# RWKV core: the transposed 32x32 blocks of the join, read off PSUM by VectorE instead of multiplied by TensorE

## The chip, the cores and the metric

The kernel runs on one core of one Trainium2 chip. The metric is the device time of one execution, in microseconds (us): the median of several runs. Five engines work side by side, each through a queue of its own in order: TensorE (PE in the profile, its weight loads are PEld), VectorE (DVE), ScalarE (ACT), GpSimd (POOL) and SyncE (SP, which here issues the transfers).

## The reference

Four layers of token mixers over 256 context and 256 latent tokens of 1024 features: retention, mLSTM, RWKV-7, retention. Only the third is touched. Its scan is, for 16 heads of 64 features and in both directions:

```python
def step(S, inp):
    rt, wt, kt, vt, at, bt = inp
    sa = jnp.einsum('bhij,bhj->bhi', S, at)
    S = S * wt[:, :, None, :] + sa[..., None] * bt[:, :, None, :] + vt[..., None] * kt[:, :, None, :]
    return S, jnp.einsum('bhij,bhj->bhi', S, rt)
```

## The kernel before

All matrices of the other layers are float32, split into two parts and multiplied three times (lines 255 to 257 of the profile). The RWKV core works on chunks of 64 tokens. Within a chunk the term with `sa` couples the tokens, so that a triangular 64x64 system stands for each head and direction; it is solved by inverting unit triangular matrices, first of 16, then of 32, then of 64 rows.

There are eight chunks per direction, so eight stages n = 0 to 7. In a stage the core handles four units (two directions, two halves of the heads), by these functions:

- `prep` (P) loads k, kk and r and makes decays and keys: `L1284` on TensorE, `L1289` to `L1296` and `L1310` on ScalarE, `L1292`, `L1293`, `L1300`, `L1301`, `L1305`, `L1307` on VectorE, the rest on GpSimd.
- `grams1` (G) multiplies keys by each other (`L1327`) and copies the diagonal 32x32 blocks into `AD` and the lower left ones into `off` (ScalarE, in the profile `AD<-g` and `q<-g`); `grams2` (H) does the same for another pair (`L1343`).
- `solve` (I) inverts the 16-row blocks of all heads at once on VectorE (`L1372` to `L1383`), and leaves them turned, as `O1` (the tile `AD`), and not turned, as `O2`.
- `whole` (J), called the join from here on, makes 32-row and then 64-row inverses. It has 16 blocks b for each of four quarters of the partitions, so each of its first steps is 64 small matmuls of 32x32. `L1394` multiplies the off-diagonal 16-row part by `O2`, `L1395` (VectorE) adds the identity and gives `Pm`. `L1399` multiplies `O1` by `Pm`: the 32-row inverse, in PSUM; four ScalarE copies (one helper line, `L1197`) put it into `M` (in the profile the tile `bdB`). `L1405` multiplies the same pair the other way round, `Pm` by `O1`: the same blocks transposed, in another PSUM bank, and a ScalarE copy makes them `MT`. `L1411` multiplies `off` by `M`; two copies, one on ScalarE and one on VectorE, make `Q` (in the profile `Pm<-ps`). `L1417` multiplies `MT` by `Q`, and two more copies complete `M`. `L1423` multiplies by `M` and gives `G`, which the steps need.
- `step` (T) advances the state of one unit: `L1438`, `L1440` and, after a copy, `L1447`, `L1449`, `L1450`.
- `ada` (A) makes the scales of the fourth layer, `L307`, in the last two stages, from weights that stream in as `adaw`.

The program text runs P, G, H, I and J of stage n, then A of stage n and T of stage n-1. The order on each engine is not the text's: a scheduler lays all instructions out on a time line of its own and sorts every engine's queue by that, so that rows of T, P, G and H stand between those of a join. An edit anywhere in the core therefore moves other rows too. The PSUM pool behind `bank("ps")` has two buffers.

The profile's records count two matmuls and two weight loads for each float32 matmul of the program, so that the 64 matmuls of one step of a join are 128 matmul records.

Of the kernel before, what the change touches and what calls it, by code (L numbers as in the profile page):

```python
# [131 lines left out]
class Net:  # L132
# [1051 lines left out]
    def rk_core(self, es, e0, K, B, xd, h, xx, p1, p0):  # L1184
        nc = self.nc
        mm = nc.tensor.matmul
# [10 lines left out]
        copy = lambda o, x: nc.scalar.activation(o, x, ACT.Copy)  # L1197
# [188 lines left out]
        def whole(units, O1, O2, los):  # L1386

            quarters = [(32 * q, slice(32 * q, 32 * q + 32)) for q in range(4)]
            part = lambda name: tl(name, 1, 16, 32)
            wide = lambda: bank("ps").rearrange("p q t -> p (q t)").rearrange("p (b t) -> p b t", t=32)  # L1390
            ps, Pm = wide(), part("Pm")
            for b in range(16):
                for o, r in quarters:
                    mm(ps[r, b], los[b // 8][r, :, b % 8], O2[r, :, b], start=True, stop=True, tile_position=(o, o))  # L1394
            nc.vector.tensor_tensor(out=Pm, in0=ps, in1=K["m16"][:, 2].unsqueeze(1).broadcast_to([128, 16, 32]), op=OP.add)  # L1395
            ps, MT = wide(), part("MT")
            for b in range(16):
                for o, r in quarters:
                    mm(ps[r, b], O1[r, :, b], Pm[r, b], start=True, stop=True, tile_position=(o, o))  # L1399
            for q, (o, r) in enumerate(quarters):  # L1400
                (vcopy if q % 2 else copy)(M[r, :, q // 2, 32 * (q % 2):32 * (q % 2) + 32], ps[r])
            ps = wide()
            for b in range(16):
                for o, r in quarters:
                    mm(ps[r, b], Pm[r, b], O1[r, :, b], start=True, stop=True, tile_position=(o, o))  # L1405
            copy(MT, ps)
            ps, Q = wide(), part("Pm")
            low = [(64 * h, slice(64 * h, 64 * h + 32), 64 * h + 32, slice(64 * h + 32, 64 * h + 64)) for h in range(2)]
            for b in range(16):
                for h, (o, r, o2, r2) in enumerate(low):  # L1410
                    mm(ps[r2, b], units[b // 4]["off"][r, b % 4], M[r, b, h, 0:32], start=True, stop=True, tile_position=(o, o2))  # L1411
            for h, (o, r, o2, r2) in enumerate(low):
                (qcopy if h else copy)(Q[r2], ps[r2])
            ps = wide()
            for b in range(16):
                for o, r, o2, r2 in low:
                    mm(ps[r2, b], MT[r2, b], Q[r2, b], start=True, stop=True, tile_position=(o2, o2))  # L1417
            for h, (o, r, o2, r2) in enumerate(low):
                (qcopy if h else copy)(M[r2, :, h, 0:32], ps[r2])
            for m, u in enumerate(units):  # L1420
                ps = bank("ps")
                for p in range(4):
                    mm(ps[:, p], cat(M[:, 4 * m + p]), u["RB"][:, p], start=True, stop=True)  # L1423
                u["G"] = tl("G", GN, 4, 128)
                (gcopy if m % 2 else copy)(u["G"], ps)
# [124 lines left out]
        def J(n, m):  # L1550
            whole(U[n], *O[n])
# [142 lines left out]
```

## Time and profile before

| | |
|---|---|
| median of 3 runs | 2121.55 us (2121.2 to 2126.33) |
| the profiled execution | 2119.65 us |
| its span, first to last instruction | 2117.9 us |
| busy: TensorE / VectorE / ScalarE / GpSimd | 93% / 60% / 43% / 20% of the span |
| the joins | eight, from 1265 us to about 1665 us of the span |

The profile says of each engine when it was busy and, for idle time, what released the instruction that ended it. "issue" as a releaser means that nothing that the profile shows was waited for. [...]

### The profile page before, as it was taken

How to read it: one execution, taken by the hardware profiler on the slowest of the kernel's cores; microseconds unless marked ns; L12 is line 12 of the kernel's file. 1: busy time of each engine (PE TensorE's matmuls, PEld its weight loads, DVE VectorE, ACT ScalarE, POOL GpSimd, SP SyncE). 2: the span in 40 equal slices, each digit the busy share in tenths (PEclk: the TensorE clock that was granted, in tenths of full speed). 3: DMA queues.
4: the chain of work that ended last, by engine and by line, in shares of the span. 5: the costliest groups of instructions: out<-in, count | busy, mean ns of one | idle time of the engine just before them, and what ended most of it. 6: DMA issues, size and time to landing. Idle time of an engine off the chain costs nothing.

```text
span 2117.9 us, 41647 instructions
## 1 busy us (share of the span) xinstructions
PE 1968.9 (93%) x17146; PEld 1676.3 (79%) x17146; DVE 1260.9 (60%) x2296; ACT 919.6 (43%) x1841; POOL 430.5 (20%) x459
## 2 busy tenths in 40 slices
PE   6999999999999989989699998999999898999996
PEld 5888887887777868777567987888898676999995
DVE  4463544446646266676867536777766466665554
ACT  3241423233434555342435436666665342444433
POOL 1000000004300143340700402332322033311001
PEclk9999999999999989999899998999999999999998
DMA  9332434331554564443135521112234630233331
GB/s 302 107 119 92 138 100 130 105 120 60 189 179 130 171 195 134 149 125 112 61 124 166 168 69 48 40 52 60 70 87 135 202 123 1 90 121 110 120 108 42
DMA packets 241550, 246.40 MB, mean 116 GB/s; under 512 B 30992, under 2 KB 200080, under 8 KB 241360
## 3 DMA queue, kind: packets, MB, share of 16 engines
q1 hardware_dynamic: 241360, 243.73, 36.8%
q8 instruction: 135, 2.21, 0.4%
q14 instruction: 55, 0.45, 0.1%
HBM read 216.29 MB, written 27.39 MB: 115 GB/s over the span
## 4 chain that ended last, share of the span: by engine, by line
PE 73%; DVE 12%; DMA 5%; ACT 5%; issue 3%; POOL 2%; SPq 0%; ACTq 0%; DVEq 0%; POOLq 0%
PE pp L255 15%; PE pp L256 15%; PE pp L257 15%; PE po L256 2%; PE ps L82 2%; PE g L1327 2%; PE po L257 2%; PE po L255 2%; PE ps L307 1%; DMA raw<-ada_w 1%; DVE wl L239 1%; PE g L1343 1%; PE pp L1450 1%; PE ps L255 1%; PE pp L1447 1%
## 5 line engine op out<-in xcount | busy, mean ns | idle before, releaser
L239 DVE TENSOR_TENSOR wl<-wraw,wh 128x1024 fp32r<-128x1024 f32 x216 | 269.3, 1248 | 196.1 <-ACT wh L237 186.7
L237 ACT ACTIVATE wh<-wraw 128x1024 fp32r<-128x1024 f32 x216 | 228.5, 1059 | 271.8 <-PE pp L256 129.0
L255 PE MATMUL pp<-hA,wh 128*128 128x512 f32 (+1 forms) x704 | 255.9, 366 | 8.1 <-DVE rp L526 3.0
L256 PE MATMUL pp<-hB,wh 128*128 128x512 f32 (+1 forms) x704 | 255.4, 364 | 0.0
L257 PE MATMUL pp<-hA,wl 128*128 128x512 f32 (+1 forms) x704 | 255.2, 364 | 0.1
L255 PE MATMUL pp<-zh,wh 128*128 128x512 f32 (+1 forms) x620 | 216.7, 352 | 6.5 <-ACT zh L287 6.0
L257 PE MATMUL pp<-zh,wl 128*128 128x512 f32 (+1 forms) x620 | 212.3, 343 | 0.0
L256 PE MATMUL pp<-zl,wh 128*128 128x256 f32 (+1 forms) x512 | 170.8, 334 | 4.4 <-DVE zl L288 2.9
L366 DVE SCALAR_TENSOR_TENSOR x<-pp,mod,x 128x256 f32<-128x256 f32 x192 | 87.0, 480 | 137.2 <-PE pp L257 136.9
L255 PEld LDWEIGHTS pp<-hA,wh 128*128 128x128 f32 x704 | 132.8, 189 | 33.1 <-PE pp L257 3.6
L257 PEld LDWEIGHTS pp<-hA,wl 128*128 128x128 f32 x704 | 133.5, 190 | 24.3 <-issue 1.6
L256 PEld LDWEIGHTS pp<-hB,wh 128*128 128x128 f32 x704 | 133.6, 190 | 22.5 <-issue 1.7
L255 PE MATMUL pp<-wh,hA 128*128 128x256 f32 x512 | 146.4, 287 | 2.0 <-ACT wh L237 1.9
L255 PEld LDWEIGHTS pp<-zh,wh 128*128 128x128 f32 x620 | 119.0, 192 | 34.1 <-ACT zh L287 6.9
L256 PE MATMUL pp<-wl,hA 128*128 128x256 f32 x512 | 145.1, 284 | 0.5 <-DVE wl L239 0.5
L257 PE MATMUL pp<-wh,hB 128*128 128x256 f32 x512 | 145.0, 284 | 0.0
L257 PEld LDWEIGHTS pp<-zh,wl 128*128 128x128 f32 x620 | 119.4, 193 | 19.3 <-issue 6.7
L256 PEld LDWEIGHTS pp<-zl,wh 128*128 128x128 f32 x512 | 99.2, 194 | 18.6 <-issue 5.4
L255 PEld LDWEIGHTS pp<-wh,hA 128*128 128x128 f32 x512 | 97.5, 191 | 5.9 <-issue 2.6
L256 PEld LDWEIGHTS pp<-wl,hA 128*128 128x128 f32 x512 | 97.4, 190 | 1.4 <-DVE wl L239 0.8
L257 PEld LDWEIGHTS pp<-wh,hB 128*128 128x128 f32 x512 | 97.5, 190 | 0.0
L288 DVE TENSOR_TENSOR vl<-pp,vh 128x256 fp32r<-128x256 f32 x64 | 26.9, 421 | 82.4 <-ACT vh L287 82.4
(520 smaller groups left out, 4687.4 us busy)
## 6 DMA issues: line engine op xcount, KB each, us to landing
wraw<-ret_w_in SPq DMA_DIRECT2D x96, 512.0 KB, 3.8
wraw<-ada_w SPq DMA_DIRECT2D x56, 512.0 KB, 4.0
wraw<-ret_w_out SPq DMA_DIRECT2D x32, 512.0 KB, 3.5
wraw<-ml_w_in SPq DMA_DIRECT2D x32, 512.0 KB, 3.8
wraw<-rk_w_rkvg SPq DMA_DIRECT2D x32, 512.0 KB, 3.7
adaw<-ada_w SPq DMA_DIRECT2D x48, 256.0 KB, 4.4
raw<-ada_w SPq DMA_DIRECT2D x16, 512.0 KB, 7.5
wraw<-ml_w_out SPq DMA_DIRECT2D x16, 512.0 KB, 4.5
```

Of the source, the lines that this page charges most:

```text
L82: nc.tensor.matmul(self.sums[32 * j:32 * j + 32, n * HALF:n * HALF + HALF], net.ones[:, 0:32], src, start=c < 4 and n == 0, stop=c >= 4 an ...
L237: nc.scalar.activation(h, t, ACT.Copy)
L239: (nc.gpsimd if self.nsplit % 4 in self.psplit else nc.vector).tensor_tensor(out=l, in0=t, in1=f(h), op=OP.subtract)
L255: mm(ps, lhs[0], rhs[0], start=start, stop=False)
L256: mm(ps, lhs[0], rhs[1], start=False, stop=False)
L257: mm(ps, lhs[1], rhs[0], start=False, stop=stop)
L288: (eng or self.nc.vector).tensor_tensor(out=l, in0=src, in1=f(h), op=OP.subtract)
L307: nc.tensor.matmul(ps[32 * j:32 * j + 32, 0:m].rearrange("p (b q) -> p b q", b=nb), self.csil[:, k, :], raws[k // n][:, k % n, j], start=k ...
L366: self.nc.vector.scalar_tensor_tensor(out=x, in0=ps, scalar=self.gate(i, c, st), in1=x, op0=OP.mult, op1=OP.add)
L1327: mm(g[:, p, 0:192], cat(u["bb"][:, p]), W[:, p], start=True, stop=True)
L1343: mm(g[:, p, 0:192], cat(u["kb"][:, p]), W[:, p], start=True, stop=True)
L1447: mm(f_[0:m, p], AK[:, p, 64:64 + m], cat(V[:, p]), start=True, stop=False)
```

## The change

The second set of 64 matmuls of each join, its PSUM bank and its ScalarE copy go. In their place one VectorE instruction reads the result of the first set from PSUM, turns each 32x32 block and writes `MT`. What `MT` holds is the same.

```diff
                     mm(ps[r, b], O1[r, :, b], Pm[r, b], start=True, stop=True, tile_position=(o, o))
             for q, (o, r) in enumerate(quarters):
                 (vcopy if q % 2 else copy)(M[r, :, q // 2, 32 * (q % 2):32 * (q % 2) + 32], ps[r])
-            ps = wide()
-            for b in range(16):
-                for o, r in quarters:
-                    mm(ps[r, b], Pm[r, b], O1[r, :, b], start=True, stop=True, tile_position=(o, o))
-            copy(MT, ps)
+            nc.vector.transpose(MT.rearrange("p b t -> p (b t)"), ps.rearrange("p b t -> p (b t)"))
             ps, Q = wide(), part("Pm")
```

Later lines move up by four: `L1411` becomes `L1407`, `L1417` `L1413`, `L1423` `L1419`, and the steps' `L1438`, `L1440`, `L1447`, `L1449`, `L1450` become `L1434`, `L1436`, `L1443`, `L1445`, `L1446`. The transpose is `L1402`. The scheduler's order changes in the whole core, and hardly outside it.

TensorE's queue at join 2, before:

```order
L1438 MATMUL pp<-bdB,AK 64x128
L1399 MATMUL ps<-Pm,AD_10515 32x32 x64
L1405 MATMUL ps<-AD_10515,Pm 32x32 x64
L1327 MATMUL g_13022<-W_11336,bdA 128x192 x4
L1440 MATMUL pp<-S_11351,W_10503 64x128
...
L1411 MATMUL ps<-bdB,q 32x32 x32
```

and now:

```order
L1327 MATMUL g_12827<-W_11336,bdA 128x192 x2
L1399 MATMUL ps<-Pm,AD_10515 32x32 x64
L1327 MATMUL g_12827<-W_11336,bdA 128x192 x2
L1434 MATMUL pp<-bdB,AK 64x128
L1436 MATMUL pp<-S_11351,W_10503 64x128
...
L1443 MATMUL pp<-bdB,AK 128x128
L1407 MATMUL ps<-bdB,q 32x32
```

The gram matmuls and the steps now follow the first block of 64 at once, and stand between it and the block that reads `M`.

TensorE's queue at join 6, before (no other row stood between the blocks there):

```order
L1284 MATMUL g_15787<-ta,ca_9162 128x128
L1399 MATMUL ps<-Pm,AD_10515 32x32 x64
L1405 MATMUL ps<-AD_10515,Pm 32x32 x64
L1411 MATMUL ps<-bdB,q 32x32 x32
L1450 MATMUL pp<-bdB,G 128x128
```

and now:

```order
L1399 MATMUL ps<-Pm,AD_10515 32x32 x64
L1443 MATMUL pp<-bdB,AK_11350 128x128
L1445 MATMUL pp<-S_11357,W_11337 128x128
L1446 MATMUL pp<-bdB,G 128x128
...
L1284 MATMUL g_15332<-ta,ca_9162 128x128
L1407 MATMUL ps<-bdB,q 32x32
L1327 MATMUL g_15371<-W_11336,bdA 128x192 x4
L1407 MATMUL ps<-bdB,q 32x32 x31
```

Twelve matmuls of a step have moved from behind `L1411` to before it; join 1 is alike, with seven.

VectorE's queue at join 2, before:

```order
L1395 TENSOR_TENSOR Pm<-ps,cm_9172 128x512
L1305 TENSOR_TENSOR bdA<-kk,em 64x4x2x64
L1453 TENSOR_TENSOR S_11357<-pp,Dc 64x4x64 x2
L1292 TENSOR_SCALAR em<-em 128x512
L1293 SCALAR_TENSOR_TENSOR em<-creset,em 128x512
L1300 SCALAR_TENSOR_TENSOR W_11337<-kk,eL_10512 128x8x64
```

and now:

```order
L1395 TENSOR_TENSOR Pm<-ps,cm_9172 128x512
L1449 TENSOR_TENSOR S_11357<-pp,Dc 64x4x64 x2
L1292 TENSOR_SCALAR em<-em 128x512
L1293 SCALAR_TENSOR_TENSOR em<-creset,em 128x512
L1402 STREAM_TRANSPOSE MT<-ps 128x512
L1300 SCALAR_TENSOR_TENSOR W_11337<-kk,eL_10512 128x8x64
```

The transpose, which waits for `L1399`, has come in ahead of the row that makes the next `W`, on which a gram waits.

## Rows read from the trace of the kernel before

**Rows 1.** The page: busy time, share of the span and instructions of each engine.

```profile
PE 1968.9 (93%) x17146; PEld 1676.3 (79%) x17146; DVE 1260.9 (60%) x2296; ACT 919.6 (43%) x1841; POOL 430.5 (20%) x459
```

**Rows 2.** Busy time by stage: start:end, length, each engine, PEclk, DMA share, GB/s.

```profile
1418.00:1474.00 56.00, 53.53 (x852) 49.34 (x848) 44.02 (x87) 37.59 (x98) 17.11 (x15) 0.94 0.22 63
sum 405.00, PE 370.16 PEld 333.85 DVE 266.48 ACT 237.41 POOL 111.64; mean PE 46.27 PEld 41.73 DVE 33.31 ACT 29.68 POOL 13.96
```

**Rows 3.** The same view, from the solve of stage 3 to its end.

```profile
1398.60:1417.80 19.20, 18.05 (x164) 16.48 (x163) 18.32 (x49) 6.51 (x19) 0.00 (x0) 1.00 0.21 57
```

**Rows 4.** Groups by line, 1265 to 1670: busy, mean ns, idle before and releasers.

```profile
L1405 PE MATMUL ps<-AD,Pm 32*32 32x32 f32 x1024 | 18.1, 229 | 12.6 <-issue 12.6
L1399 PE MATMUL ps<-Pm,AD 32*32 32x32 f32 x1024 | 16.5, 222 | 1.2 <-issue 0.8 <-DVE Pm L1395 0.3
L1411 PE MATMUL ps<-bdB,q 32*32 32x32 f32 x512 | 11.7, 207 | 7.1 <-ACT bdB L1197 6.5 <-issue 0.6
L1197 ACT ACTIVATE MT<-ps 128x512 f32<-128x512 f32 x8 | 4.8, 597 | 3.0 <-PE ps L1405 2.7
```

**Rows 5.** TensorE's time line at joins 2 and 5: start, length, row, idle before.

```profile
1376.62 2.02 PE L1399 MATMUL ps<-Pm,AD 32*32 32x32 f32 x128
1378.46 1.42 PE L1405 MATMUL ps<-AD,Pm 32*32 32x32 f32 x84
1381.52 0.85 PE L1405 MATMUL ps<-AD,Pm 32*32 32x32 f32 x44 [1.65 <-issue]
1382.30 2.69 PE L1327 MATMUL g<-W,bdA 128*128 128x192 f32 x8
...
1393.27 1.57 PE L1327 MATMUL g<-W,bdA 128*128 128x192 f32 x8 [0.26 <-ACT RB L1197]
...
1537.20 0.76 PE L1405 MATMUL ps<-AD,Pm 32*32 32x32 f32 x38
...
1540.69 0.80 PE L1450 MATMUL pp<-bdB,G 128*128 128x128 f32 x2
```

**Rows 6.** Windows of 1 us after that gap (columns as in Rows 2).

```profile
1382.00:1383.00 1.00, 1.00 (x27) 0.91 (x16) 0.64 (x1) 0.93 (x3) 0.94 (x2) 0.79 0.73 219
1383.00:1384.00 1.00, 1.00 (x5) 1.00 (x4) 1.00 (x3) 0.61 (x2) 0.84 (x2) 0.50 0.00 0
...
1386.00:1387.00 1.00, 1.00 (x16) 0.83 (x16) 0.00 (x0) 0.97 (x4) 0.00 (x0) 1.00 0.00 0
```

**Rows 7.** The page: the instruction queue with the most bytes.

```profile
q8 instruction: 135, 2.21, 0.4%
```

**Rows 8.** TensorE's time line at join 7, and around the lone block of join 4.

```profile
1641.88 1.95 PE L1399 MATMUL ps<-Pm,AD 32*32 32x32 f32 x122 [0.83 <-issue]
...
1647.00 2.02 PE L1405 MATMUL ps<-AD,Pm 32*32 32x32 f32 x123 [3.10 <-issue]
...
1474.33 2.23 PE L1394 MATMUL ps<-O,q 32*32 32x32 f32 x128 [1.00 <-DVE O L1383]
...
1477.68 0.27 PE L1450 MATMUL pp<-bdB,G 128*128 128x128 f32 x1 [0.81 <-issue]
```

**Rows 9.** TensorE and ScalarE at join 0 and join 1.

```profile
1280.59 1.92 PE L1411 MATMUL ps<-bdB,q 32*32 32x32 f32 x64 [4.26 <-ACT bdB L1197]
1334.37 1.66 PE L1411 MATMUL ps<-bdB,q 32*32 32x32 f32 x64 [1.45 <-ACT bdB L1197]
1331.94 2.37 ACT L1197 ACTIVATE bdB<-ps 32x512 f32<-32x512 f32 x4
```

**Rows 10.** Groups by line on VectorE: transposes and a copy out of PSUM.

```profile
L1382 DVE STREAM_TRANSPOSE AD<-LS 128x1024 f32<-128x1024 f32 x7 | 8.7, 1245 | 0.2
L1383 DVE STREAM_TRANSPOSE O<-LS 128x1024 f32<-128x1024 f32 x7 | 13.4, 1914 | 0.0
L310 DVE STREAM_TRANSPOSE lnt<-g 128x128 f32<-128x128 f32 x6 | 1.9, 310 | 5.0 <-PE g L307 5.0
L1198 DVE COPY G<-ps 128x512 f32<-128x512 f32 x15 | 10.2, 680 | 6.5 <-PE ps L1423 6.5
```

## The prediction

> **What bounds the kernel now.** I read the page first: TensorE is busy 93% of the span [rows 1]. The change lies in the eight joins alone, so next comes the view by stage: over the 405 us that hold them TensorE is busy 370 us, VectorE 266 and ScalarE 237 [rows 2]; in stage 3 it is 53.5 of 56 us for TensorE and 44 for VectorE. A microsecond taken from TensorE's queue there should shorten the stage unless VectorE's solve sets the pace. It does for one stretch: between the first instruction of the solve and its end, 19.2 us, VectorE is busy 18.3 us [rows 3], and the block L1394 that follows it can wait for it (1.00 us at join 4) [rows 8]. But the solve starts from grams that stand behind the join before it in TensorE's queue, so a shorter join starts it earlier as well.
>
> Then the groups by line. L1405, which the change removes, is busy 18.1 us in all and has 12.6 us of idle time before or inside it that nothing visible ends, "issue" [rows 4]. Its twin L1399 has only 1.2 us. The time line of join 2 shows what that is: L1399 runs 128 records in 2.02 us, L1405 runs 84, stops for 1.65 us, and runs the other 44 [rows 5]. [...] L1327 x8 takes 2.69 us there and 1.57 us ten microseconds later at full clock [rows 5].
>
> **What the gap is.** The page counts 17146 matmuls and 17146 loads [rows 1], and 135 packets with 2.21 MB on one instruction queue [rows 7]: 254 records and 16.4 KB a packet. Two blocks of 64 in a row are 512 records. At join 7 the engine stops inside L1399 and again inside L1405, with 122 matmuls, one more and five between (and as many loads): one packet apart [rows 8]. The small matmuls eat a packet in some 1.9 us, and the next is not there. The lone block L1394 has such a gap in one join of eight, two matmuls behind its end, 0.81 us [rows 8]; there it fills a packet almost exactly. So I take the gap as a cost of two blocks in a row, and expect it to go where one is left, except when the one fills a packet. [...]
>
> **The change part by part.**
>
> *TensorE, joins 2 to 5.* From the start of L1405 to the start of the next instruction, gap included: 1382.30 - 1378.46 = 3.84 us at join 2 [rows 5]; read in the same way the last of the four, join 5, has 1540.69 - 1537.20 = 3.49 us [rows 5], and the two between have 3.8 and 3.1. Sum 14.2. Counted by the groups it is the same: four eighths of 16.5 to 18.1 us are 8.3 to 9.0, and the four gaps, from 1.65 at join 2 to 1.25 at join 5, make 5.4 of the 12.6. Here other work stood between L1405 and L1411, M's copies were long done, and all of it is on TensorE's path. By the count of records in the new queue, L1399 of join 5 fills a packet almost exactly, so I keep 0.8 of gap there: **13.4**.
>
> *The clock.* After the gap 0.21/0.50 + 3 = 3.4 us at half clock [rows 6], of which half is lost, 1.7 us. The same view has 3.4 us at half clock behind the gaps of joins 3 and 4. In join 5 the clock was already low from an earlier wait, so I count three: **5.1**. It goes only if no new idle time comes in the gap's place.
>
> *Joins 1 and 6.* Here L1411 follows directly and waits for M's four copies on ScalarE: at join 1 until 1334.3, 1.45 us [rows 9], at join 6 0.84 us, the rest of the 6.5 us of [rows 4] beside join 0. Taking L1405 away alone would give nothing, since ScalarE gets to the copies when it does. What helps is the new order: seven matmuls at join 1, of which four are L1327 (1.57 us [rows 5]) and three have 128 columns instead of 192 (so some 0.2 each), and twelve such short ones at join 6, move into the hole: 2.2 and 2.4 us, of which I take **4.2**.
>
> *Join 0.* L1411 waits 4.26 us for copies that stand behind the preparation on ScalarE [rows 9]; they still stand there in the new queue. The same filling would give 3 us, but the copies of Q now stand behind more of the next preparation: I take **1.0**, bounds 0 and 3.
>
> *Join 7.* L1405 (2.0) and its gap (3.10) [rows 8] lie in a stage that also waits for the streamed ada weights. Bounds 0 and 5; I take **2.0**.
>
> *ScalarE* loses eight copies of 597 ns, 4.8 us [rows 4]. It is idle four tenths of the time; nothing is counted.
>
> *VectorE* gains eight transposes of 128x512 from PSUM. No row has that shape. From 128x128 out of PSUM (310 ns) and 128x1024 (1245 ns) [rows 10] a straight line gives 710 ns; half of the 128x1024 is 620, half of the one that writes with a stride 960; a plain copy of the shape out of PSUM is 680. I take 0.7 us, nearest to the copy, 5.6 us in all, bounds 5 and 7.7. It does not stand in the solve's stretch. It reads the bank that ScalarE copies at the same time; the two have no wait on each other. MT is wanted only by L1417, behind L1411 and Q's copies, so the transpose itself is covered by those. What it holds up is VectorE's queue: at join 2 the W, and after it the grams, stand behind it, as shown with the change. Against them I put half of its length, 0.35 us a join, **-2.8**. And the new order moves rows in every stage: where a copy is late now, TensorE waits, and if long enough the clock falls as above. Eight joins, one such loss of about 1.2 us among them: **-1.2**.
>
> Sum: 13.4 + 5.1 + 4.2 + 1.0 + 2.0 - 2.8 - 1.2 = **21.7 us**. What follows the core, the fourth layer, starts as much earlier; its transfers go by buffers that come free, so they move along. The profiled execution took 2119.65 us, 1.9 below the median, so 2098 there and 2121.55 - 21.7 = **2100** for the median.
>
> **The rivals.**
>
> *The gaps stay.* If they belong to the pace of instructions and not to the pair of blocks, they move to the end of L1399, and the clock falls with them. Then joins 2 to 5 give 8.7 instead of 13.4, and the 5.1 is gone: 21.7 - 9.8 = 12, **2109.5**. For it: join 7 has a gap inside L1399 too. Against it: L1394, a block of the same size that stands alone, has one in eight. [...]
>
> *The gain is eaten by waits of the copies.* In five joins less work stands between L1407 and L1413 than stood between L1411 and L1417, while Q still goes through a ScalarE and a VectorE copy, one after the other. Each time that TensorE stops for a microsecond there costs that and 1.7 for the clock. With 2.3 us lost per join (18.4 in all), 3.3 of the gain is left: **2118**. For it: joins 0, 1 and 6 wait for copies today [rows 4]. Against it: ScalarE has less to do and in joins 2 to 5 did not make TensorE wait.
>
> *Slower: the transpose holds up the solve.* It waits for L1399 in VectorE's queue, ahead of W, kk and bdA of the next unit. If L1399 runs late, those, the grams, AD's copies and the solve, which has no slack of its own [rows 3], come late by as much, and L1394 waits. With w us per join the loss is 8w; above 21.7/8 = 2.7 us the kernel is slower, and with w = 4 it is 2121.55 - 21.7 + 32 = **2132**. Against it: in the queue of join 2 the scan L1293 stands ahead of the transpose, so that the transpose is not the first thing that the next W waits for.
>
> **How the numbers follow.** Forecast (14.5 to 31 us gained) 0.58; gaps stay (7 to 14.5) 0.18; eaten by waits 0.13; slower 0.06; more than 31 us, because the clock stays up in all joins (1.7 each in joins 0 and 1), 0.05. With every unknown at its better bound (2 more at join 0, 3 more at join 7, nothing lost on VectorE or to new order, 4.0) 30.7 us are gained, and with the clock up in two more joins 34: 2087. The range runs from there through the first rival to 2117, and leaves the slower case and most of the third outside. A measurement of this kernel tells some 0.3%, 6.4 us, from no change. Faster than that 0.81, within it 0.13, slower 0.06.
>
> **What would show it.** Right: no "issue" gap behind L1399 in six or more joins, and at most 2 us of them in all; granted clock 1.00 behind L1399 in joins 2 to 4; the transpose at 0.62 to 0.75 us; the stages 1 to 6 each 2 to 5 us shorter; the span from 1670 on unchanged in length. Wrong: gaps at the end of L1399; L1407 or L1413 waiting for copies by a microsecond or more in several joins; L1394 waiting for O by more than today's 2.4 us in all; VectorE idle at L1402 while W is late.

## The result, and the profile after

The kernel after takes 2103.52 us (4 runs, 2100.83 to 2105.34), beside 2123.94 us of the kernel before on the same chip: ratio 0.9897, 95% interval 0.9876 to 0.9918, so 20.4 us less. A second group gave 2103.51 us and 0.9905 (0.9879 to 0.9930). I had said 2100, between 2087 and 2117.

The page of the profile of after, busy time by engine and the instruction queue, answers to [rows 1] and [rows 7]:

```profile
PE 1956.7 (93%) x16122; PEld 1663.6 (79%) x16122; DVE 1269.5 (60%) x2304; ACT 918.8 (44%) x1835; POOL 429.8 (20%) x459
...
q8 instruction: 127, 2.08, 0.4%
```

1024 matmul records and as many loads are gone, and 8 packets with them: 256 records for each. I call the stretch from the first join's L1394 to the last matmul of the last step the core. By stretch, before (columns as in [rows 2], where PEclk is TensorE's granted clock as a share of full speed; joins 0 and 1, joins 2 to 5, then joins 6 and 7 with the last steps):

```profile
1265.64:1370.21 104.57, 90.68 (x1570) 82.36 (x1569) 66.99 (x137) 65.86 (x171) 32.82 (x35) 0.89 0.19 51
1370.21:1585.38 215.17, 204.53 (x3383) 187.48 (x3383) 158.00 (x319) 137.40 (x352) 62.99 (x60) 0.94 0.23 65
1585.38:1703.41 118.03, 103.77 (x1896) 90.62 (x1895) 64.58 (x132) 50.85 (x118) 18.36 (x21) 0.94 0.50 158
```

and after:

```profile
1264.47:1367.42 102.95, 91.20 (x1318) 82.19 (x1317) 68.15 (x138) 64.36 (x169) 33.35 (x35) 0.85 0.19 51
1367.42:1579.25 211.83, 195.71 (x2859) 177.54 (x2858) 163.62 (x324) 137.87 (x350) 62.84 (x60) 0.97 0.24 66
1579.25:1686.38 107.13, 100.75 (x1646) 88.40 (x1645) 63.52 (x132) 49.77 (x114) 18.36 (x21) 0.94 0.54 169
```

The core fell from 437.8 to 421.9 us, and these 15.9 us are most of the 18.8 between the two profiled executions; 1.2 lie ahead of the core and 1.8 behind it. Only 3.3 of them lie in joins 2 to 5, where I had put most of the gain: TensorE is busy 8.8 us less there, and idle 5.5 us more. The largest part, 10.9 us, lies at the end.

The groups by line of after, 1265 to 1660, answer to [rows 4]:

```profile
L1327 PE MATMUL g<-W,bdA 128*128 128x192 f32 x224 | 52.3, 385 | 9.5 <-DVE bdA L1305 6.5 <-ACT RB L1197 3.0
L1399 PE MATMUL ps<-Pm,AD 32*32 32x32 f32 x1024 | 16.7, 217 | 2.1 <-issue 1.8 <-DVE Pm L1395 0.3
L1407 PE MATMUL ps<-bdB,q 32*32 32x32 f32 x512 | 13.1, 206 | 3.0 <-ACT bdB L1197 3.0
L1413 PE MATMUL ps<-Pm,MT 32*32 32x32 f32 x512 | 11.9, 198 | 5.8 <-ACT Pm L1197 5.2 <-DVE Pm L1198 0.5
L1402 DVE STREAM_TRANSPOSE MT<-ps 128x512 f32<-128x512 f32 x8 | 5.7, 710 | 7.2 <-ACT bdB L1197 7.1
```

The 12.6 us of "issue" at the removed line are gone, and 18.1 us of work with them. L1327 has waits that it did not have: it stood at 0.7 us of idle time before (in the same view), and is at 9.5 now. (`bdA` is the operand of the grams that VectorE and GpSimd make in halves; `RB` is copied from a gram's result, in part by ScalarE.) TensorE's time line of after shows where gaps are left, and the longest new waits:

```profile
1272.52 1.87 PE L1434 MATMUL pp<-bdB,AK 128*64 128x128 f32 x8 [1.47 <-issue]
...
1287.92 0.31 PE L1413 MATMUL ps<-Pm,MT 32*32 32x32 f32 x2 [3.69 <-ACT Pm L1197]
...
1383.23 0.43 PE L1434 MATMUL pp<-bdB,AK 128*64 128x128 f32 x2 [2.10 <-ACT bdB L1197]
...
1383.50 0.38 PE L1436 MATMUL pp<-S,W 128*64 128x128 f32 x2
...
1384.38 0.63 PE L1436 MATMUL pp<-S,W 128*64 128x128 f32 x2
...
1425.57 2.93 PE L1327 MATMUL g<-W,bdA 128*128 128x192 f32 x8 [3.02 <-DVE bdA L1305]
...
1539.03 0.24 PE L1399 MATMUL ps<-Pm,AD 32*32 32x32 f32 x2 [1.01 <-issue]
```

At join 2, where the gap of [rows 5] was, TensorE now waits 2.10 us for a copy of a step, and a microsecond later L1436 x2 takes 0.63 us where it took 0.38: the granted clock is 1.00 until 1384, 0.68 in the microsecond from there and 0.50 in the next two, as it fell to 0.50 behind the gap [rows 6]. At join 3 the wait is 3.02 us, the clock is at 0.50 from 1426 to 1428, and L1327 x8 takes 2.93 us, where it took 1.57 at full clock [rows 5].

The trace also has each packet of the instruction queue, with its start and its length. These times say more on the gaps than the count does. At join 2 before, a packet of 16 KB came in from 1378.86 to 1380.01; TensorE stopped at 1379.87 and went on at 1381.52 [rows 5]. All twelve "issue" waits of the core before, and all five of after, end 1.2 to 1.5 us behind the end of such a packet; over this stretch of all fourteen profiles it is 89 of 89, at 1.2 to 1.6 us. On average a packet comes every 8.0 us in the core before and every 9.3 after, so by chance few would. The gaps are waits for the next packet: this is shown, not only counted.

### The profile page after: what moved, and what is told of

It reads as the page before. It is cut to its first block, busy times and chain, and to the rows that moved or that the text cites. A ratio compares the mean times of both kernels' runs of the same rounds, so it can differ in the third digit from the quotient of the medians.

```text
span 2099.1 us, 39601 instructions
## 1 busy us (share of the span) xinstructions
PE 1956.7 (93%) x16122; PEld 1663.6 (79%) x16122; DVE 1269.5 (60%) x2304; ACT 918.8 (44%) x1835; POOL 429.8 (20%) x459
## 4 chain that ended last, share of the span: by engine, by line
PE 74%; DVE 12%; ACT 5%; DMA 4%; issue 3%; POOL 2%; SPq 0%; ACTq 0%; DVEq 0%; POOLq 0%
PE pp L255 16%; PE pp L256 16%; PE pp L257 16%; PE ps L82 2%; PE po L256 2%; PE po L257 2%; PE g L1327 2%; PE po L255 2%; PE g L1343 2%; DMA raw<-ada_w 2%; DVE wl L239 1%; PE ps L307 1%; PE ps L1419 1%; ACT AD L1197 1%; PE ps L255 1%
## 5 line engine op out<-in xcount | busy, mean ns | idle before, releaser
L257 PE MATMUL pp<-zh,wl 128*128 128x512 f32 (+1 forms) x620 | 211.8, 342 | 0.0
```

The costliest lines, as they stand in the source:

```text
L257: mm(ps, lhs[1], rhs[0], start=False, stop=stop)
```

## The experiments

Each is compared with the kernel before as it ran in the same group; those medians lie between 2122.2 and 2124.1 us.

**The block put back, unread.** The kernel after, with the second block of 64 behind the transpose; nobody reads its result.

```diff
             nc.vector.transpose(MT.rearrange("p b t -> p (b t)"), ps.rearrange("p b t -> p (b t)"))
+            ps = wide()
+            for b in range(16):
+                for o, r in quarters:
+                    mm(ps[r, b], Pm[r, b], O1[r, :, b], start=True, stop=True, tile_position=(o, o))
             ps, Q = wide(), part("Pm")
```

> The changed kernel with the second block of 64 matmuls put back in each join, its result read by nobody: MT still comes from the VectorE transpose, the ScalarE copy stays away. In the new queue the block follows the first one directly in all eight joins. If the gain is TensorE's time (the block's 1.84 us and the idle gap that goes with two blocks in a row), nearly all of it goes: 14.7 us and about 11 us of gaps come back, less what other waits hid, 2120 to 2130 us, with 10 us or more of issue gaps. If the gain came from the ScalarE copy that is gone or from the new order, it stays at 2101 to 2109.

Measured 2132.36 us, ratio 1.0045 (1.0027 to 1.0064). The gain goes entirely with the block, though ScalarE's copies stay away and the transpose stays: neither of these brings the gain while the block is there. The gaps are back as well; the waits of TensorE in the core say

```profile
PE ps L1406 <- issue: 13.9, 8, 2.8
```

(us in all, times, longest). That it is 10 us slower than the kernel before was in no theory; the scheduler had again made another order, so this run alone does not price the block.

**Half of the block.** The kernel before, with the transposed product only for the two quarters that L1417 reads.

```diff
-                for o, r in quarters:
+                for o, r in quarters[1::2]:
                     mm(ps[r, b], Pm[r, b], O1[r, :, b], start=True, stop=True, tile_position=(o, o))
-            copy(MT, ps)
+            for o, r in quarters[1::2]:
+                copy(MT[r], ps[r])
```

> The kernel before, with the transposed product computed only for the two of four quarters that L1417 reads: 32 matmuls instead of 64 in each join, and two ScalarE copies of 32 partitions instead of one of 128. 32 such matmuls on two quarters take 1.20 us in L1411 at join 2 against 1.84 us for the 64, so 0.6 us per join goes, 5 us; two blocks in a row are then 384 records instead of 512. If the gap comes where a whole packet of 256 records lies in such blocks, it becomes rarer and shorter, and half or more of the 12.6 us goes: 2108 to 2116 us in all. If every second block costs a gap whatever its length, only the 5 us go, less two more copies on ScalarE: 2117 to 2122.

Measured 2110.15 us, ratio 0.9938 (0.9916 to 0.9960). 12 of the 20 us come with half of the matmuls, and the gaps fall from 12.6 us in eight joins to 4.0 in three. They depend on the length of the run of small matmuls, as the packet theory wants it. (The order moved in this run and the next too.)

**The transpose beside the block.** The kernel before, with the VectorE transpose added; the ScalarE copy then writes over it.

```diff
+            nc.vector.transpose(MT.rearrange("p b t -> p (b t)"), ps.rearrange("p b t -> p (b t)"))
```

> The kernel before, with the VectorE transpose added in each join: it writes MT, and the ScalarE copy of the second product then writes the same values over it. So it has the cost of the transpose in VectorE's queue alone. By the prediction's term of 2.8 us: 2123 to 2128. If the transpose holds up the preparation and the solve behind it, 2.7 us or more per join: above 2140. If it is covered wholly: 2120 to 2123.

Measured 2122.92 us, ratio 0.9998 (0.9984 to 1.0011): eight transposes in VectorE's queue cost nothing that can be told.

**Packets shifted.** The kernel after, with 25 repeated matmuls in the first product of the program, 100 records.

```diff
+            for _ in range(25 if i == 0 and p == 0 else 0):
+                nc.tensor.matmul(ps[0:32, 0:m].rearrange("p (b q) -> p b q", b=nb), self.csil[:, 0, :],
+                                 raws[0][:, 0, 0], start=True, stop=True, tile_position=(0, 0))
```

> The changed kernel with 25 repeated matmuls in the first ada product at the start of the program, far from the joins, which waits for transfers there. They put 100 more records ahead of everything, so that the ends of the 256-record packets fall elsewhere in every join. Counted from the gaps of the kernel before, L1399 begins 88, 118, 192, 52, 170, 104, 70 and 46 records behind a packet's start in joins 0 to 7, where it was 244, 18, 92, 208, 70, 4, 226 and 202. If a gap comes when the packet is nearly filled by one block, as in joins 0 and 5 of the changed kernel, none stands behind or in L1399 in joins 0 to 6, issue gaps in the core fall from 4.9 to under 2 us, and the time is 2097 to 2103 us, with some spread from a slightly different order. If the gaps belong to these joins and not to the packets, they stay at joins 0, 5 and 7 with 4 to 6 us.

Measured 2115.46 us, ratio 0.9962 (0.9943 to 0.9981). The gaps at joins 0 and 5 went, as said; 3.5 us of "issue" were left where under 2 were expected, 0.9 at L1394 of join 6 and 2.6 at join 7. And the time was 12 us above the kernel after, against the expectation. The scheduler's order had moved too, so this did not tell gaps from order. Hence the runs that follow, in which every engine's queue is held in an order that is written into the kernel.

**Program and order crossed.** Behind the program's text, each instruction is tied to the one that is to stand before it on its engine (an order, no wait). The heart of it, without the list `order`:

```diff
+    for k in order:
+        i = t[k]
+        if i.engine in last:
+            tc.add_manual_dep(i, last[i.engine].name, info, reason="order")
+        last[i.engine] = i
```

First the program after in the order of before, the transpose where the copy stood:

> The program after the change, but with every engine's queue held in the order of the kernel before: the second block and its copy are simply left out, and the transpose stands where that copy stood in the scheduler's list. Nothing else moves. Theory (the gain is the block and its gaps): the block and gaps behind L1399 of joins 2 to 5 (some 13 us) and of join 7 (up to 5) go, joins 0, 1 and 6 give little since L1407 then waits for M's copies; transposes cost 0.7 as in the run with both; so 14 to 20 us faster than before: 2102 to 2108. Rival (the new order brings the gain, by the steps that fill the wait for M's copies): the wait L1407 <- copies of M grows by 1.5 us a join and the time is 2112 or more.

Then the program before in the order of after, the second block directly behind the first:

> The program before the change, but in the order of the kernel after, with the second block of 64 directly behind the first, and its copy where the transpose stood. Theory (gain is the block and its gaps, order neutral): 2119 to 2126, as before. Rival 1 (the new order is itself better by the 2 to 4 us that I put on joins 1 and 6): 2114 to 2119. Rival 2 (the new order is itself worse, which the run with an unread second block pointed to): 2127 to 2133.

Measured 2115.53 us (0.9951, 0.9932 to 0.9970) and 2126.10 us (1.0002, 0.9987 to 1.0016). By stretch, in us of the profiles:

| | before | after's program, before's order | before's program, after's order | after |
|---|---|---|---|---|
| joins 0, 1 | 104.6 | 103.1 | 105.7 | 103.0 |
| joins 2 to 5 | 215.2 | 212.4 | 224.3 | 211.8 |
| joins 6, 7, last steps | 118.0 | 116.0 | 115.7 | 107.1 |
| core | 437.8 | 431.5 | 445.7 | 421.9 |
| median (after: its own group) | 2124.1 | 2115.5 | 2126.1 | 2103.5 |

In before's order the change is worth 6.3 us of the core, in after's 23.8; the order by itself brings nothing (2126.1 us against 2124.1, and a core longer by 7.9). Neither the block nor the order brings the 20 us alone. Much of why before's order keeps so little is in TensorE's waits there:

```profile
PE ps L1407 <- ACT bdB L1197: 15.0, 7, 7.2
PE ps L1407 <- issue: 4.2, 1, 4.2
```

and at join 0, on its time line:

```profile
1269.91 2.02 PE L1399 MATMUL ps<-Pm,AD 32*32 32x32 f32 x128
1279.13 0.31 PE L1407 MATMUL ps<-bdB,q 32*32 32x32 f32 x2 [7.19 <-ACT bdB L1197]
```

The wait for M's copies was 6.5 us [rows 4], 4.26 of them at join 0 [rows 9]; now it is 15.0, and 7.19 at join 0. Block and gap had covered 8.5 us of waiting. In after's order it is 3.0. Of the 15.0 us, 14.1 stand at joins 0, 1 and 6 and only 1.0 in joins 2 to 5. It is what the prediction said of joins 1 and 6, that to take L1405 away alone gives nothing there; and with the order held, the rival "the gain is eaten by waits of the copies" comes near (2118 forecast, 2115.5 measured), though by M's copies more than by Q's. The second line, 4.2 us at join 7, is a wait for a packet again, behind a block that stands alone.

**Packets shifted, order held.**

> The kernel after in exactly its own order, with 27 repeated matmuls at the program's start (some 2 us of work, hidden behind the first weights or not), which move the packet boundaries by 108 records: L1399 then starts 96, 126, 200, 60, 178, 112, 78 and 54 records into a packet. Packet theory: the gaps behind L1399 at joins 0 and 5 (1.47 and 1.01 us) are gone and no other appears there; with the clock that they pulled down, 2 to 7 us less in the core; the time 2097 to 2104. Rival (the last shift cost 12 us by itself, through the boundaries and not through the changed order): 2110 to 2118.

Measured 2106.15 us, ratio 0.9915 (0.9894 to 0.9936). No gap is left at joins 0 to 6, which shows the packet count right (join 7 keeps 3.3 us); yet no time is gained, and the core is 429.5 us, beside 421.9 and (in the repeat) 423.9. So the 12 us of the first shift were the order for the most part, and something else eats what the gaps gave; the profiles say more than that, but the intervals of the medians overlap. Join 4 shows one piece. After, VectorE at `finish` (L1486) and the next unit's `em` (L1292), and GpSimd's row:

```profile
1483.59 0.69 DVE L1486 TENSOR_TENSOR Y<-Y,mu 128x512 f32<-128x512 f32 x1
1484.20 1.51 DVE L1292 TENSOR_SCALAR em<-em 128x512 f32<-128x512 f32 x1
```

```profile
1483.61 1.82 POOL L1319 TENSOR_TENSOR th<-th,r 128x512 f32<-128x512 f32 x1
```

The same rows with the shift (lines three higher):

```profile
1479.36 1.81 DVE L1489 TENSOR_TENSOR Y<-Y,mu 128x512 f32<-128x512 f32 x1
1481.09 0.41 DVE L1295 TENSOR_SCALAR em<-em 128x512 f32<-128x512 f32 x1
```

```profile
1479.35 1.27 POOL L1322 TENSOR_TENSOR th<-th,r 128x512 f32<-128x512 f32 x1
```

In the one, VectorE starts 0.02 us ahead of GpSimd and takes 0.69 us; in the other 0.01 us behind it and takes 1.81. What follows on ScalarE (a square of Y, then M's and Q's copies) comes 1.1 us later in the stage, and L1413 waits 2.65 instead of 1.55 us. In each of the two it is the row that starts second which is longer than in the other run: VectorE's with 1.81 instead of 0.69 us, GpSimd's with 1.82 instead of 1.27. VectorE's `em` row is alike: after, L1292 starts 0.59 us behind the start of GpSimd's row and takes 1.51 us; with the shift it starts 0.47 us behind that row's end and takes 0.41. What makes these rows longer no run here shows.

**Transposes twice, order held.**

```diff
             nc.vector.transpose(MT.rearrange("p b t -> p (b t)"), ps.rearrange("p b t -> p (b t)"))
+            nc.vector.transpose(MT.rearrange("p b t -> p (b t)"), ps.rearrange("p b t -> p (b t)"))
```

> The kernel after in exactly its own order, with each transpose issued twice, one behind the other (0.7 us more in VectorE's queue per join, 5.7 us in all). If the transposes are covered (slack in VectorE's queue): within 1.5 us of the kernel after, 2102 to 2106. By my term of half a length each: 2.8 us more, 2106 to 2108. If VectorE's queue has no slack behind L1399: 5.7 us or more, with clock losses up to 10: 2109 to 2114.

Measured 2108.46 us (2102.31 to 2112.51), ratio 0.9918 (0.9899 to 0.9937). The intervals overlap with those of the kernel after; the core is 420.8 us, not longer, but the profiled execution was the fastest of the six. The profile says covered, the median would allow 5 us: unclear, but the profile shows no sign of a queue without slack.

**Copies first.** The kernel after in its own order, with copies moved ahead in ScalarE's queue, and one in VectorE's, at places of waits like those shown above.

> The kernel after in its own order, but for eight places in ScalarE's queue and one in VectorE's where a copy for which TensorE waited stood behind work that nobody waited for yet: at joins 0 and 4 the ScalarE copy of Q (at join 0 VectorE's too) and a step's copies go ahead of the grams' copies AD; at join 2 a step's copies; at join 3 M's four copies ahead of the square root's table load; at joins 2 and 4 an RB copy one gram ahead; at join 7 a step's copies and one G ahead of the split of a weight that is still in transit. TensorE's queue is untouched. Theory (the new waits are ScalarE's order, no lack of ScalarE time): of the 15.5 us of waits at these places two thirds go, with some clock: 8 to 14 us faster than the kernel after, 2090 to 2096. Rival (the waits move on to the next copy, or to VectorE's rows of the next unit): 2099 to 2106.

Measured 2106.30 us, ratio 0.9918 (0.9905 to 0.9932), no gain. At joins 0 and 2 the waits shrank, but VectorE's next unit took their place. TensorE's largest wait in the core is

```profile
PE g L1327 <- DVE bdA L1305: 11.3, 6, 3.0
```

against 6.5, 4, 3.0 after. With the packets shifted as well:

> The same with the 27 repeated matmuls at the program's start, which keep L1399 clear of a packet's end. If the gaps at joins 0 and 5 cost what they show and nothing else moves: 2 to 5 us under the run with the copies first. If a coincidence of VectorE and GpSimd like the one at join 4 of the shifted run comes with it (there a row of VectorE took 1.81 instead of 0.69 us, and TensorE lost 2.6 us): equal to that run or up to 8 us above it.

Measured 2107.92 us, ratio 0.9934 (0.9920 to 0.9947); this wait stands at 14.1 us there. A gap removed is again not time gained.

**Three places.** Of those moves only the ones at joins 0, 2 and 7, whose stretches had become shorter; in the same group the kernel after once more.

> Of the moves of the run with the copies first, only those at joins 0, 2 and 7 (there stages 0 and 2 were 1.5 and 2.0 us shorter than in the kernel after, and what follows join 7 0.9), not those at join 4 (stage 4 was 3.4 us longer) and join 3 (0.3). Theory (what a move gives is local to its stage): the core, from the first join's first block to the last step, 3.5 to 4.5 us shorter than 421.6, some 417.5; the time, beside the repeat of the kernel after in the same group, 3 to 5 us lower. Rival (each move changes which row of VectorE meets which of GpSimd in later stages, and so the later stages are drawn anew): core between 418 and 426, the time within 4 us of the kernel after on either side.

> The kernel after, unchanged, in the same group as the run before it. If its first median stands for it, 2101 to 2106 (ratio 0.988 to 0.992), and the twice-issued transposes (2108.5, in another group) cost 3 to 5 us; if 2107 or more, they cost nothing that can be told.

Measured 2098.90 us (2094.79 to 2103.70), ratio 0.9884 (0.9860 to 0.9907), and 2103.51 us (2098.41 to 2106.56), ratio 0.9905 (0.9879 to 0.9930). The first is the lowest median of all, 4.6 under the kernel after as expected, but the intervals overlap, and the core is 419.8 us where I had expected 417.5: 2.1 less than after's first profile (421.9; the 421.6 of the expectation began 0.3 us late), 4.1 less than its second. Faster than the kernel before is shown; faster than the kernel after is likely, not shown. The repeat came out in the range in which, as I had written, the transposes issued twice would cost 3 to 5 us; their interval overlaps with the repeat's too, so that cost stays unclear.

## Why the prediction was right, and where it was not

The number was 3.5 us off, and the gain 20.4 where 21.7 was forecast. The terms were further off, in both directions.

- *The gaps belong to two blocks in a row.* Right. In the core the "issue" waits of TensorE fell from 15.7 to 4.8 us. What was left stood at join 5, where I had kept 0.8 (1.01, two records before the block's end), at join 0 (1.47), at join 7 (2.1) and, 0.3, behind L1394 of join 1. By the count of records L1399 starts 244, 18, 92, 208, 70, 4, 226 and 202 records into a packet of 256, and the two that nearly fill one are joins 0 and 5; with the shift these went. Five joins are free, not six, and the sum is above the 2 us that I had allowed. The rival "the gaps stay" is out. At join 7 the pair of blocks is not the condition: there TensorE waits for packets in or behind a block that stands alone too, 2.1 us after and 5.1 in before's order. Why they come late there is open.
- *Joins 2 to 5, 13.4 us.* The work and the gaps went as forecast: 9.1 us of block, and the waits for packets fell from 6.2 to 1.0. But the stretch became only 3.3 us shorter, and 2.7 in before's order. The step that failed is "all of it is on TensorE's path". TensorE's waits other than "issue" there grew from 4.2 us to 15.1, and to 14.9 in before's order: the block and its gaps had covered other engines. M's copies, of which I had said that they were long done, are little of it (L1407 waits 1.5 us after and 1.0 in before's order). Most of it is waits for `bdA` and Y from VectorE and for `RB`, `Pm` and copies for the steps from ScalarE. The longest waits of joins 2 to 5, before:

```profile
PE ps L1405 <- issue: 5.4, 4, 1.6
PE ps L1394 <- DVE O L1383: 2.4, 3, 1.2
```

after's program in before's order:

```profile
PE pp L1443 <- DVE Y L1459: 3.8, 2, 2.0
PE g L1327 <- DVE bdA L1305: 3.3, 1, 3.3
PE ps L1413 <- ACT Pm L1197: 2.7, 2, 2.4
```

and after:

```profile
PE g L1327 <- DVE bdA L1305: 3.9, 2, 3.0
PE g L1327 <- ACT RB L1197: 3.0, 2, 1.7
PE pp L1434 <- ACT bdB L1197: 2.7, 2, 2.1
```

With the block put back in after's order the four stages are 12.5 us longer than without it. That is near 13.4, but by another sum: 9.1 us of block and 8.0 of gaps more, 7.6 of other waits less, and other rows 2.9 longer.
- *The clock, 5.1 us.* It did not come where I had put it. I had written that it goes only if no new idle time comes in the gap's place, and that came: 2.10 us at join 2, 3.02 at join 3, 1.07 at join 4, each with the granted clock at 0.50 behind it (1385 to 1387, 1426 to 1428, 1484 to 1486). It came back elsewhere. In joins 2 to 5 the granted clock is 0.97 on average and was 0.94, for the most part by join 5, where it had been low for 10 us. That stage before and after:

```profile
1529.73:1585.38 55.65, 53.68 (x904) 49.33 (x905) 36.28 (x77) 32.81 (x84) 14.21 (x15) 0.91 0.30 83
1530.98:1579.25 48.27, 46.04 (x741) 41.29 (x740) 35.95 (x76) 31.04 (x80) 14.93 (x14) 1.00 0.35 98
```

At joins 0 and 1 it is lower, 0.85 and was 0.89. Counted as time at half clock, the core has 58 us (55 in the repeat), and had 65. What that is worth is not shown: in joins 2 to 5 TensorE's busy time fell by 8.8 us, no more than the block's 9.1.
- *The new order, 4.2 us at joins 1 and 6 and 1.0 at join 0.* Right in kind, too small, and not where I had put it. The waits for M's copies are 15.0 us in before's order and 3.0 in after's, and the core differs by 9.6 us between these two. But 8.9 of these lie in the last stretch alone (116.0 to 107.1), and at joins 0 and 1, where they fell by 10 us, nothing is left of it (103.1 to 103.0): L1413 waits 3.7 us there instead, L1327 2.7, packets cost 1.8, and TensorE's rows are 4.5 us longer, at a lower clock.
- *VectorE and new waits, -4.0.* TensorE's waits other than "issue" grew in the core from 22.8 to 29.0 us, 6.2. The other rows of TensorE became longer too, by 6.8 us (18.1 us of block went, busy time fell by 11.3), 5.0 of them at joins 0 and 1 with their lower clock: L1327 stands at 385 ns instead of 368. Nothing shows that the transposes themselves are part of that (0.7 us each as said; what doubling them, or adding them to before, costs can't be told from noise). One sentence on them was false, that the two readers of the bank have no wait on each other: the transpose waits for ScalarE's four copies, 7.1 us in all, at joins 0, 6 and 7; at join 0, ScalarE's copies and VectorE's row:

```profile
1276.99 2.40 ACT L1197 ACTIVATE bdB<-ps 32x512 f32<-32x512 f32 x4
```

```profile
1279.42 0.72 DVE L1402 STREAM_TRANSPOSE MT<-ps 128x512 f32<-128x512 f32 x1 [2.53 <-ACT bdB L1197]
```

- *The sum.* In the core 18.1 us of block and 10.9 of gaps went, 29.0; 6.2 of waits and 6.8 of slower rows came; 15.9 are left. My sum had 20.6 of removal and filling, 5.1 of clock and 4.0 of loss. Two misses of 8 to 9 us, more removed and more lost, cancelled: that the number is near is luck in good part.
- *What would show it.* L1394 waits for O by 0.4 us or more in no join, so the rival on the slow side, a solve held up, is out. L1407 or L1413 wait by a microsecond or more at two joins only. The granted clock is 1.00 behind L1399 at joins 2 and 3 and falls 1.6 us behind its end at join 4. Stages 1 to 6 are not each 2 to 5 us shorter: between the starts of L1394 they took 47.1, 47.6, 56.5, 55.4, 55.6 and 50.8 us before, and 47.1, 51.4, 55.2, 57.0, 48.3 and 56.2 after. Matmuls of the steps changed stage (188 records to 148 in stage 5, 134 to 204 in stage 6), so a single stage is not the same work on both sides; joins 2 to 5 together differ by 8 records of some 620. What follows the core is 1.8 us shorter (414.5 to 412.7); kernels that are alike there spread from 412.7 to 418.8, so this part is not explained.

Left open: what a transpose ahead of M's copies would give was not tried. With the order held, the block was never put back without its ScalarE copy, so that the two are not priced apart there. Each kernel but after has one profile, and after's two differ by 2.0 us in the core: smaller differences between cores say nothing. Nor do the runs say why the unread block cost 10 us beyond the kernel before, but for its order.

## What to carry to other kernels

Work that is removed from the busiest engine is worth what it did not cover (here 29.0 us of block and gaps went, and the core became 15.9 us shorter): look, row by row, at which copy or operand of another engine would be late if it were gone, and whether the scheduler has other rows to put there. Hold the order when an edit is to be priced; here the same edit was worth 6 us of the core in one order and 24 in another. Add up work, gaps and waits apart, since a total that fits can hide two misses. The second blocks of 64 tiny matmuls cost twice here, 18.1 us by their time and 12.6 by waits for instruction packets [rows 4], and half of the block taken away brought 12 of the 20 us, more than half.

## What the hardware showed unexpectedly

Two things beside the gaps. Where a VectorE row and a GpSimd row met at join 4, start times 0.02 and 0.01 us apart went with which of them was long: VectorE's took 0.69 us when it started first and 1.81 when second, GpSimd's 1.27 and 1.82. Where both make halves of `bdA`, at join 3 after, VectorE's two rows took 3.42 us, beside 1.39 at join 0; this is the 3.02 us wait of L1327 shown above. VectorE, then GpSimd:

```profile
1422.10 3.42 DVE L1305 TENSOR_TENSOR bdA<-kk,em 64x512 f32<-64x512 f32 x2
```

```profile
1421.94 1.36 POOL L1312 TENSOR_TENSOR th<-th,k 128x512 f32<-128x512 f32 x1 [5.32 <-ACT th L1310]
1423.38 3.27 POOL L1317 TENSOR_TENSOR bdA<-th,em 64x512 f32<-64x512 f32 x2
```

And the clock falls at different places in two executions of one program. Stage 1 in windows of 10 us from the same point of the work, first profile of after:

```profile
1330.00:1340.00 10.00, 7.80 (x94) 6.36 (x96) 6.59 (x8) 9.70 (x23) 9.51 (x8) 0.66 0.19 56
1340.00:1350.00 10.00, 9.39 (x123) 8.82 (x120) 4.11 (x8) 8.25 (x25) 2.48 (x3) 1.00 0.00 0
```

and its repeat:

```profile
1326.10:1336.10 10.00, 6.25 (x128) 4.93 (x128) 6.61 (x8) 9.70 (x23) 9.53 (x8) 0.98 0.19 56
1336.10:1346.10 10.00, 9.71 (x74) 9.28 (x70) 2.10 (x5) 7.62 (x23) 2.48 (x3) 0.67 0.00 0
```

In the first the half clock falls on a stretch in which TensorE waits anyway (7.8 of 10 us busy), in the second on one in which it is busy nearly throughout (9.7); stage 1 took 47.1 and 49.1 us.
